# Decay rows of the state-space scan: transposed once per layer and read back from DRAM, in place of four transposes per head

## The chip, the cores and the metric

The kernel runs on one core of one Trainium2 chip. The metric is the time of one execution in microseconds, as the median of several runs. A core has TensorE (matrix multiplication, results in PSUM), VectorE, ScalarE, GpSimd and SyncE. Here SyncE issues every data transfer; 16 DMA engines carry them out. TensorE reads SBUF and writes PSUM, and GpSimd's work in this kernel is all on SBUF.

## What is computed

Two layers of a decoder trunk. Each layer projects its input once, sends parts of the projection through three branches (latent attention, a delta-rule recurrence, a state-space scan), gates and adds the branches, and ends with a feed-forward block. The change lies in the scan:

```python
a_cs = jnp.cumsum(da, axis=-1)                 # running decay sums per head
decay_in = jnp.exp(segsum(da))                 # exp(a_cs[l] - a_cs[s]) for l >= s
cb = jnp.einsum('bclgn,bcsgn->bgcls', cm, bm)
y_diag = jnp.einsum('bgcls,bgecls,bcsgep->bclgep', cb, decay_in, x)
```

There are 16 heads of 64 channels in 2 groups and 512 tokens. The kernel takes all 512 tokens as one chunk.

## The kernel before

Tokens are handled in four chunks of 128 (NC4 = 4, P = 128, S = 512). Products with weights are made from three passes each: every weight tile `wraw` of 512 KB is loaded by SyncE, rounded by ScalarE into `wH` (L231), and VectorE keeps the remainder in `wL` (L232); a projection (`proj`, L265, tile `pj`) is 24 matmuls of 512 columns. There are two raw buffers and three of each split.

In the stage of interest `mixer` interleaves three generators by a fixed pattern (`PAT`): `ssm` (the scan), `mla_attn` (attention: scores `sc`, softmax `P`, transposes `pT`, output `o`) and `gate` projections; after the attention the scan goes on beside the merging of the other branches (`rest`, `merge_two`: tiles `of`, `oH`, `oL`, `br`, `th`).

`ssm_dt` computes the step sizes and the decays on small tiles of 128 tokens x 4 chunks x 16 heads; its last product is the running sum, which L964 copies into `y` (the trace calls the tile `dy`; its negative is `de`). `ssm` then works on pairs of heads: `scores(g)` makes for each group the matrix `CB` from two convolved projections (`Bm`, `Cm`); `decays(i)` convolves a projection to `xs`, transposes it (`xT`, L1014) and scales it into `X` (L1016), and for each of the two heads builds the decay matrix `E`: running sums along the free axis, on all partitions (`ab`, L1023 to L1025), a minimum with the sum of the row's own token (L1028, VectorE), four exponentials of 128 columns (L1030) and three of 384, 256 and 128 (L1033) on ScalarE, and the product with `CB` (L1036: VectorE for the first head of a pair, GpSimd for the second). There are three buffers `E`. `out(i)` multiplies `E` with `X` on TensorE (`y`, L1049), then gates the result with another projection (`z`) and sums squares on GpSimd (L1058, L1064).

The rows `ab` come from `bcast_rows`: a column of 128 tokens, repeated along the free axis by its access pattern, goes through a TensorE transpose (L280), which leaves the column as a row on all 128 partitions in PSUM. That is four transposes for a head. The PSUM pool of the scan has three banks.

The order of the instructions on each engine is made by a planner when the program is built: it goes by the order of the program text and by its own estimates of when operands and buffers are ready, so instructions of different generators are interleaved. SyncE's transfers are in such an order too, and an instruction whose operands are not ready holds up all behind it on its engine.

Of the kernel before, what the change touches and what calls it, by code (L numbers as in the profile page):

```python
# [8 lines left out]
F32 = mybir.dt.float32  # L9
# [8 lines left out]
P = 128  # L18
S = 512
D = 1024  # L20
KD = D // P
NC4 = S // P
# [33 lines left out]
class Kern:  # L56
# [875 lines left out]
    def ssm_dt(self, T):  # L932

        nc = self.nc
        ps = self.pss.tile([P, S], F32, name="dtT", tag="r")
        for c in range(NC4):
            nc.tensor.transpose(out=ps[:, 16 * c:16 * c + 16], in_=self.krd[32:48, c * P:(c + 1) * P],
                                identity=self.ident[32:48, 32:48])
        x, e, u, y, g = (T(n, [P, NC4, 16]) for n in ("dx", "de", "du", "dy", "dg"))
        hb = lambda j: self.hrow[:, j:j + 1, :].to_broadcast([P, NC4, 16])  # L940
        nc.vector.tensor_tensor(out=x, in0=ps[:, 0:64].rearrange("p (c h) -> p c h", c=4), in1=hb(0), op=ALU.add)

        nc.vector.scalar_tensor_tensor(out=u, in0=x, scalar=-1.0, in1=x, op0=ALU.mult, op1=ALU.max)
        nc.scalar.activation(out=e, in_=u, func=AF.Exp, scale=-1.0)
        nc.vector.tensor_scalar(out=u, in0=e, scalar1=2.0, scalar2=None, op0=ALU.add)
        nc.vector.reciprocal(out=u, in_=u)
        nc.vector.tensor_tensor(out=e, in0=e, in1=u, op=ALU.mult)
        nc.vector.tensor_tensor(out=y, in0=e, in1=e, op=ALU.mult)
        nc.vector.tensor_scalar(out=g, in0=y, scalar1=1.0 / 15, scalar2=1.0 / 13, op0=ALU.mult, op1=ALU.add)
        for n in (11, 9, 7, 5, 3, 1):  # L950
            nc.vector.tensor_tensor(out=g, in0=g, in1=y, op=ALU.mult)
            nc.vector.tensor_scalar(out=g, in0=g, scalar1=1.0 / n, scalar2=None, op0=ALU.add)
        nc.vector.tensor_tensor(out=g, in0=g, in1=e, op=ALU.mult)
        nc.vector.tensor_scalar(out=x, in0=x, scalar1=0.0, scalar2=None, op0=ALU.max)
        nc.vector.scalar_tensor_tensor(out=x, in0=g, scalar=2.0, in1=x, op0=ALU.mult, op1=ALU.add)
        nc.vector.tensor_tensor(out=u, in0=x, in1=hb(1), op=ALU.mult)
        nc.vector.tensor_scalar(out=x, in0=x, scalar1=0.5, scalar2=None, op0=ALU.mult)
        ps = self.pss.tile([P, S], F32, name="acs", tag="r")
        nc.vector.memset(g[:, 0], 0.0)
        for c in range(1, NC4):  # L960
            nc.vector.tensor_tensor(out=g[:, c], in0=g[:, c - 1], in1=u[:, c - 1], op=ALU.add)
        for i, (m, t) in enumerate(((self.mle, u), (self.ones128, g))):
            nc.tensor.matmul(out=ps[:, 0:64], lhsT=m, rhs=t.rearrange("p c h -> p (c h)"), start=i == 0, stop=i == 1)
        nc.vector.tensor_copy(out=y, in_=ps[:, 0:64].rearrange("p (c h) -> p c h", c=4))  # L964
        nc.vector.tensor_scalar(out=e, in0=y, scalar1=-1.0, scalar2=None, op0=ALU.mult)
        return x, y, e

    def conv_silu(self, pg, j, out):
# [15 lines left out]
    def ssm(self, T):  # L984
        nc, l = self.nc, self.l
        PS = lambda name: self.pss.tile([P, S], F32, name=name, tag="r")
        pg = lambda name, bufs=2: T(name, [P, S], bufs)
        off = [S, S + 384, S + 640]
        dth, acs, nacs = self.ssm_dt(T)
        CB, X, xs, E, ys = {}, {}, {}, {}, {}  # L990

        def scores(g):
            Bm, Cm = pg("Bm", 1), pg("Cm", 1)
            self.conv_silu(pg, 8 + g, Bm)
            yield
            self.conv_silu(pg, 10 + g, Cm)
            cb = CB[g] = T(f"CB{g}", [P, 1280])
            for k in range(NC4):
                w = S - k * P
                ps = PS("cb")  # L1000
                nc.tensor.matmul(out=ps[:, 0:w], lhsT=Bm[:, k * P:(k + 1) * P], rhs=Cm[:, k * P:S], start=True, stop=True)
                nc.vector.scalar_tensor_tensor(out=cb[:, k * P:(k + 1) * P], in0=ps[:, 0:P], scalar=0.25, in1=self.mle,
                                               op0=ALU.mult, op1=ALU.mult)
                if k < 3:
                    nc.scalar.activation(out=cb[:, off[k]:off[k] + w - P], in_=ps[:, P:w], func=AF.Copy, scale=0.25)
            yield

        def decays(i):
            g = i // 4
            x = xs[i] = pg("xs")  # L1010
            self.conv_silu(pg, i, x)
            ps = PS("xT")
            for c in range(NC4):
                nc.tensor.transpose(out=ps[:, c * P:(c + 1) * P], in_=x[:, c * P:(c + 1) * P], identity=self.ident)  # L1014
            X[i] = T("X", [P, NC4, 2, 64], 2)
            nc.vector.tensor_tensor(  # L1016
                out=X[i].rearrange("p c h n -> p c (h n)").rearrange("p c (h n) -> p c h n", h=2),
                in0=ps.rearrange("p (c h n) -> p c h n", c=4, h=2),
                in1=dth[:, :, 2 * i:2 * i + 2].rearrange("p c (h o) -> p c h o", o=1).to_broadcast([P, NC4, 2, 64]), op=ALU.mult)
            E[i] = []  # L1020
            for hp in range(2):
                h = 2 * i + hp
                pa = PS("ab")  # L1023
                for c in range(NC4):
                    self.bcast_rows(pa[:, c * P:(c + 1) * P], acs[:, c, h:h + 1])  # L1025
                e = T("E", [P, 1280], EB)
                v4 = lambda t: t[:, 0:S].rearrange("p (c t) -> p c t", c=NC4)
                nc.vector.tensor_tensor(out=v4(e), in0=v4(pa), in1=acs[:, :, h:h + 1].to_broadcast([P, NC4, P]), op=ALU.min)  # L1028
                for k in range(NC4):
                    nc.scalar.activation(out=e[:, k * P:(k + 1) * P], in_=e[:, k * P:(k + 1) * P], func=AF.Exp,  # L1030
                                         bias=nacs[:, k, h:h + 1])
                for k in range(3):
                    nc.scalar.activation(out=e[:, off[k]:off[k] + S - (k + 1) * P], in_=pa[:, (k + 1) * P:S], func=AF.Exp,  # L1033
                                         bias=nacs[:, k, h:h + 1])
                eng = nc.gpsimd if hp else nc.vector
                eng.tensor_tensor(out=e, in0=e, in1=CB[g], op=ALU.mult)  # L1036
                E[i].append(e)
            yield
# [28 lines left out]
        def normed(g):  # L1067
# [6 lines left out]
            for j in range(4 * g, 4 * g + 4):  # L1074
                nc.vector.scalar_tensor_tensor(out=ys[j], in0=ys[j], scalar=self.dv[:, 30 + j:31 + j], in1=pb,
                                               op0=ALU.mult, op1=ALU.mult)
                nc.sync.dma_start(out=self.od["ssm"][j], in_=ys[j])

        yield from scores(0)
        yield from decays(0)  # L1080
        for i in range(8):
            if i == 3:
                yield from scores(1)
            if i < 7:
                yield from decays(i + 1)
            if i == 4:
                normed(0)
            yield from out(i)
# [281 lines left out]
```

## Time and profile before

| | |
|---|---|
| median of 3 runs | 2142.03 us (2141.42 to 2143.43) |
| the profiled execution | 2140.08 us, span of the profile 2138.1 us |
| TensorE busy | 2076.2 us, 97% |
| VectorE, ScalarE, GpSimd busy | 63%, 43%, 15% |
| mean DMA rate | 109 GB/s |

Times in the profile are counted from the start of its span. PE is TensorE's matmuls, PEld its weight loads, DVE is VectorE, ACT ScalarE, POOL GpSimd, SPq the queue of SyncE. A row of a group gives instructions of one line and form; `a<-b` names the tile written and the tiles read. The chain that ended last is followed back from the last instruction, at each step to what released it or to the instruction before it on its engine. Matmuls overlap: the time from the start of one to the start of the next is less than a matmul's own duration.

### The profile page before, as it was taken

How to read it: one execution, taken by the hardware profiler on the slowest of the kernel's cores; microseconds unless marked ns; L12 is line 12 of the kernel's file. 1: busy time of each engine (PE TensorE's matmuls, PEld its weight loads, DVE VectorE, ACT ScalarE, POOL GpSimd, SP SyncE). 2: the span in 40 equal slices, each digit the busy share in tenths (PEclk: the TensorE clock that was granted, in tenths of full speed). 3: DMA queues.
4: the chain of work that ended last, by engine and by line, in shares of the span. 5: the costliest groups of instructions: out<-in, count | busy, mean ns of one | idle time of the engine just before them, and what ended most of it. 6: DMA issues, size and time to landing. Idle time of an engine off the chain costs nothing.

```text
span 2138.1 us, 30818 instructions
## 1 busy us (share of the span) xinstructions
PE 2076.2 (97%) x12104; PEld 1650.6 (77%) x12104; DVE 1343.9 (63%) x2290; ACT 926.3 (43%) x1594; POOL 328.2 (15%) x240
## 2 busy tenths in 40 slices
PE   8999999999999999999999999999999999999999
PEld 6777777677778888888877777777677788888887
DVE  6886887877666543443557878777775654444434
ACT  5445534664433433333344454356644334333332
POOL 1001020212212111111111011002123111111120
PEclk9999999999999999999999999999999999999999
DMA  5331333124364232322332322322333632222332
GB/s 189 103 110 63 102 114 112 50 86 131 127 223 128 89 101 99 99 97 92 124 119 77 113 74 87 124 82 70 104 133 109 226 123 94 94 99 99 99 97 90
DMA packets 95616, 232.67 MB, mean 109 GB/s; under 512 B 17744, under 2 KB 27088, under 8 KB 95472
## 3 DMA queue, kind: packets, MB, share of 16 engines
q1 hardware_dynamic: 95472, 230.71, 33.1%
q8 instruction: 95, 1.56, 0.3%
q14 instruction: 49, 0.40, 0.1%
HBM read 197.64 MB, written 33.03 MB: 108 GB/s over the span
## 4 chain that ended last, share of the span: by engine, by line
PE 72%; DVE 11%; ACT 4%; issue 3%; DMA 2%; POOL 1%; SPq 0%; DVEq 0%; ACTq 0%; POOLq 0%
PE pj L265 35%; PE pf L265 16%; PE br L265 6%; PE wo L265 4%; DVE wL L232 2%; PE y L1049 2%; PE sc L898 1%; PE up L265 1%; ACT wH L231 1%; PE pT L916 1%; DMA wraw<-in_w 1%; PE YS L647 1%; DMA of<-o_ssm 1%; DVE CW L599 1%; PE o L924 1%
## 5 line engine op out<-in xcount | busy, mean ns | idle before, releaser
L265 PE MATMUL pj<-hH,wH 128*128 128x512 f32 (+1 forms) x1536 | 615.5, 401 | 7.4 <-ACT hH L234 7.4
L265 PE MATMUL pj<-hL,wH 128*128 128x512 f32 (+1 forms) x1536 | 613.0, 399 | 0.2
L265 PE MATMUL pj<-hH,wL 128*128 128x512 f32 (+1 forms) x1536 | 611.5, 398 | 0.9 <-DVE wL L232 0.9
L231 ACT CAST wH<-wraw 128x1024 fp32r<-128x1024 f32 (+1 forms) x314 | 327.4, 1043 | 655.3 <-PE pj L265 288.3
L232 DVE TENSOR_TENSOR wL<-wraw,wH 128x1024 fp32r<-128x1024 f32 (+1 forms) x314 | 415.1, 1322 | 143.2 <-ACT wH L231 142.8
L265 PEld LDWEIGHTS pj<-hH,wH 128*128 128x128 f32 (+1 forms) x1536 | 290.4, 189 | 73.9 <-ACT hH L234 7.4
L265 PEld LDWEIGHTS pj<-hL,wH 128*128 128x128 f32 (+1 forms) x1536 | 290.8, 189 | 65.0 <-issue 4.6
L265 PEld LDWEIGHTS pj<-hH,wL 128*128 128x128 f32 (+1 forms) x1536 | 290.2, 189 | 65.7 <-issue 3.3
L265 PE MATMUL pf<-uH,wH 128*128 128x512 f32 x512 | 199.2, 389 | 0.0
L265 PE MATMUL pf<-uL,wH 128*128 128x512 f32 x512 | 199.2, 389 | 0.0
L265 PE MATMUL pf<-uH,wL 128*128 128x512 f32 x512 | 199.2, 389 | 0.0
L333 POOL TENSOR_TENSOR u<-u,rsb 128x512 f32<-128x512 f32 x64 | 111.5, 1743 | 496.2 <-ACT u L332 474.5
L348 DVE TENSOR_TENSOR x<-x,pf 128x512 f32<-128x512 f32 x128 | 88.1, 688 | 139.0 <-PE pf L265 136.9
L232 DVE TENSOR_TENSOR uL<-u,uH 128x512 fp32r<-128x512 f32 x64 | 44.1, 692 | 138.1 <-ACT uH L231 138.1
L265 PEld LDWEIGHTS pf<-uH,wH 128*128 128x128 f32 x512 | 96.1, 188 | 20.0
L265 PEld LDWEIGHTS pf<-uH,wL 128*128 128x128 f32 x512 | 96.1, 188 | 20.0
L265 PEld LDWEIGHTS pf<-uL,wH 128*128 128x128 f32 x512 | 96.1, 188 | 19.9
L265 PE MATMUL br<-oH,wH 128*128 128x512 f32 x256 | 102.0, 399 | 6.4 <-ACT oH L231 6.4
L265 PE MATMUL br<-oL,wH 128*128 128x512 f32 x256 | 101.9, 398 | 4.3 <-DVE oL L232 4.3
L1036 POOL TENSOR_TENSOR E<-E,CB 128x1280 f32<-128x1280 f32 x16 | 48.7, 3045 | 353.5 <-ACT E L1033 310.7
L265 PE MATMUL br<-oH,wL 128*128 128x512 f32 x256 | 101.1, 395 | 0.0
L335 ACT ACTIVATE u<-u 128x512 f32<-128x512 f32 x64 | 40.5, 633 | 119.1 <-POOL u L333 119.1
(364 smaller groups left out, 2820.9 us busy)
## 6 DMA issues: line engine op xcount, KB each, us to landing
wraw<-in_w SPq DMA_DIRECT2D x302, 512.0 KB, 3.4
gd<-gt SPq DMA_DIRECT2D x48, 256.0 KB, 2.1
th<-gd SPq DMA_DIRECT2D x16, 512.0 KB, 3.9
xd<-x SPq DMA_DIRECT2D x8, 512.0 KB, 5.8
o_ssm<-ys SPq DMA_DIRECT2D x16, 256.0 KB, 2.1
x<-xd SPq DMA_DIRECT2D x8, 512.0 KB, 5.8
of<-o_ssm SPq DMA_DIRECT2D x16, 256.0 KB, 4.3
t<-gd SPq DMA_DIRECT2D x16, 256.0 KB, 2.7
```

Source lines behind the costliest of these rows:

```text
L231: nc.scalar.copy(out=H, in_=src)
L232: nc.vector.tensor_tensor(out=Lo, in0=src, in1=H.bitcast(F32), op=ALU.subtract)
L265: nc.tensor.matmul(out=ps, lhsT=ww if w_is_lhs else aa, rhs=aa if w_is_lhs else ww, start=first and k == 0 and q == 0, stop=last and k == ...
L333: nc.gpsimd.tensor_tensor(out=u, in0=u, in1=self.rsb, op=ALU.mult)
L335: nc.scalar.activation(out=u2, in_=u, func=AF.Square)
L348: nc.vector.tensor_tensor(out=xk, in0=xk, in1=ps, op=ALU.add)
L599: nc.vector.tensor_tensor(out=CW[o, hp], in0=pv[o], in1=mk, op=ALU.mult)
L647: nc.tensor.matmul(out=pS[m, 256 * hp + i * 64:256 * hp + i * 64 + 64], lhsT=LT[h, hp, i, m], rhs=Z[h, hp, i], start=True, stop=True)
L898: nc.tensor.matmul(out=ps[:, 0:w], lhsT=fT[0][:, j * P:w], rhs=fT[1][:, 0:w], start=True, stop=True)
L916: nc.tensor.transpose(out=ps[:, (j - k) * P:(j - k + 1) * P], in_=Pj[hp][j][:, k * P:(k + 1) * P], identity=self.ident)
L1036: eng.tensor_tensor(out=e, in0=e, in1=CB[g], op=ALU.mult)
L1049: nc.tensor.matmul(out=py[64 * hp:64 * hp + 64, t0:t1], lhsT=X[i][:, k, hp, :], rhs=m, start=k == 0, stop=(d == 0), skip_group_check=True)
```

## The change

`ssm_dt` also transposes the running sums, `y`, once per layer: four transposes of 128 tokens x 16 heads give a tile of 16 x 512 in PSUM; ScalarE copies it to SBUF, into one of the two buffers of the convolution's tile `cy`, and SyncE stores it to DRAM as `acd`. `decays(i)` begins with two loads that each read one row of `acd` and repeat it on all 128 partitions (256 KB written per load), into one of three buffers `ar`; the four transposes for each head are gone, and the minimum and the exponentials of L1033 read `ar` in SBUF instead of PSUM. The two tiles `CB0` and `CB1` become one tile `CB` with one buffer, which both groups use in turn.

```diff
@@ ssm_dt
         nc.vector.tensor_scalar(out=e, in0=y, scalar1=-1.0, scalar2=None, op0=ALU.mult)
+
+        ps = self.pss.tile([P, S], F32, name="aT", tag="r")
+        for c in range(NC4):
+            nc.tensor.transpose(out=ps[0:16, c * P:(c + 1) * P], in_=y[:, c, :], identity=self.ident)
+        at = T("cy", [P, S], 2)[0:16]
+        nc.scalar.copy(out=at, in_=ps[0:16])
+        self.acd = self.dram.tile([16, S], F32, name=f"acd{self.l}")
+        nc.sync.dma_start(out=self.acd, in_=at)
         return x, y, e
@@ scores
-            cb = CB[g] = T(f"CB{g}", [P, 1280])
+            cb = CB[g] = T("CB", [P, 1280])
@@ decays
             x = xs[i] = pg("xs")
+            rows = [T("ar", [P, S], 3) for _ in range(2)]
+            for hp in range(2):
+                h = 2 * i + hp
+                nc.sync.dma_start(out=rows[hp], in_=self.acd[h:h + 1].to_broadcast([P, S]))
             self.conv_silu(pg, i, x)
@@ decays, for each head
-                pa = PS("ab")
-                for c in range(NC4):
-                    self.bcast_rows(pa[:, c * P:(c + 1) * P], acs[:, c, h:h + 1])
+                pa = rows[hp]
                 e = T("E", [P, 1280], EB)
```

## Rows read from the trace of the kernel before

**Rows 1.** The page: busy us by engine (share, instructions); the chain by engine.
```profile
PE 2076.2 (97%) x12104; PEld 1650.6 (77%) x12104; DVE 1343.9 (63%) x2290; ACT 926.3 (43%) x1594; POOL 328.2 (15%) x240
...
PE 72%; DVE 11%; ACT 4%; issue 3%; DMA 2%; POOL 1%; SPq 0%; DVEq 0%; ACTq 0%; POOLq 0%
```

**Rows 2.** Windows, the scan's two stretches: busy us (instructions), clock, DMA share, GB/s.
```profile
340.00:600.00 260.00, 252.94 (x1359) 191.00 (x1358) 196.88 (x358) 143.19 (x317) 52.82 (x27) 1.00 0.30 97
1420.00:1660.00 240.00, 233.42 (x1268) 175.33 (x1267) 179.67 (x341) 135.93 (x308) 52.68 (x26) 1.00 0.29 95
```

**Rows 3.** Tile ab: count, min/median/max ns, first and last start, forms.
```profile
L280 PE MATMUL ab<-ident,dy x128: 272/273/273, 367.5 to 1629.3; 128*128 128x128 f32 x128
L1033 ACT ACTIVATE E<-ab,de x96: 350/458/572, 370.2 to 1635.8; 128x384 f32<-128x384 f32 x32, 128x256 f32<-128x256 f32 x32, 128x128 f32<-128x128 f32 x32
```

**Rows 4.** Timeline of TensorE around one group: start us, us, instruction.
```profile
405.32 1.04 PE L280 MATMUL ab<-ident,dy 128*128 128x128 f32 x8
406.20 1.02 PE L898 MATMUL sc<-kh,qh 96*128 96x512 f32 x2
```

**Rows 5.** Chain that ended last, first and last group of transposes: start us, us.
```profile
405.49 0.87 PE ab L280 x8
...
1628.66 0.87 PE ab L280 x8
```

**Rows 6.** Chain at layer 0's first pair.
```profile
368.40 0.61 DVE E L1028
...
374.56 2.41 DVE P L905
```

**Rows 7.** Tile E: the exponentials from SBUF, whole span.
```profile
L1030 ACT ACTIVATE E<-E,de x128: 384/388/407, 369.0 to 1634.6; 128x128 f32<-128x128 f32 x128
```

**Rows 8.** Chain at layer 0's sixth pair.
```profile
511.11 0.69 DVE E L1028
...
515.71 2.58 DVE E L1036
```

**Rows 9.** Timeline of VectorE: sums written and first minima, layer 0, then layer 1.
```profile
357.57 0.21 DVE L964 COPY dy<-acs 128x64 f32<-128x64 f32 x1
...
368.32 1.28 DVE L1028 TENSOR_TENSOR E<-ab,dy 128x512 f32<-128x512 f32 x2
...
1432.80 0.22 DVE L964 COPY dy<-acs 128x64 f32<-128x64 f32 x1
...
1435.24 1.28 DVE L1028 TENSOR_TENSOR E<-ab,dy 128x512 f32<-128x512 f32 x2
```

**Rows 10.** Layer 1's first pair: timeline of GpSimd, then the chain on TensorE.
```profile
1440.65 2.88 POOL L1036 TENSOR_TENSOR E<-E,CB 128x1280 f32<-128x1280 f32 x1 [72.23 <-ACT E L1033]
...
1446.17 1.01 PE y L1049 x6
```

**Rows 11.** A ScalarE copy (timeline); DMA issues: count, KB each, median us to landing.
```profile
361.27 0.58 ACT L891 COPY qh<-qh 96x512 f32<-96x512 f32 x1
...
gd<-gt SPq DMA_DIRECT2D x48, 256.0 KB, 2.1
of<-o_ssm SPq DMA_DIRECT2D x16, 256.0 KB, 4.3
o_rwkv<-o SPq DMA_DIRECT2D x16, 128.0 KB, 2.2
```

**Rows 12.** Waits of SyncE's queue, 1420 to 1660 us: total us, times, longest.
```profile
SPq L241 <- DVE wL L232: 128.2, 19, 31.5
```

**Rows 13.** Chain of layer 1 where it passes a weight load.
```profile
1596.70 4.97 DMA wraw<-in_w
```

**Rows 14.** VectorE alone and beside GpSimd products (timelines; GpSimd's second from the chain).
```profile
365.69 0.69 DVE L982 SCALAR_TENSOR_TENSOR xs<-th,cy 128x512 f32<-128x512 f32 x1
1441.47 2.61 DVE L982 SCALAR_TENSOR_TENSOR xs<-th,cy 128x512 f32<-128x512 f32 x1
...
1590.53 3.45 POOL E L1036
1591.08 0.67 DVE L1127 SCALAR_TENSOR_TENSOR th<-th,br 128x512 f32<-128x512 f32 x1
```

## Prediction

> **What bounds the kernel now.** I read the busy table of the page first. TensorE is busy for 97% of the span, and 72% of the chain that ended last lies on it; ScalarE has 4% of the chain against 43% busy [rows 1]. Then the two stretches that hold the scan, one in each layer: TensorE is busy 252.9 of 260 us and 233.4 of 240 us, VectorE about three quarters, the DMA engines 30% [rows 2]. So work taken from TensorE should shorten the stage, unless its work there is partly waiting for another engine. The other three views are the row of the removed instructions, the chain step by step, and the order of the SyncE queue.
>
> **The transposes that go.** There are 128 of them, 8 for each of the 8 head pairs in each of 2 layers, 273 ns each [rows 3]; 128 x 0.273 = 34.9 us looks like the prize and is not, because matmuls overlap. The timeline shows what a group of 8 occupies: it starts at 405.32 and TensorE starts the next work at 406.20, 0.88 us later [rows 4]. So 16 groups hold TensorE for about 16 x 0.88 = 14.1 us at most. On the chain that ended last the program's own pieces are 0.87 us a group, and only 11 of the 16 groups are on it, the first at 405.49 and the last at 1628.66 [rows 5]: 11 x 0.87 = **-9.6 us**. The other five lie beside a chain on other engines: at layer 0's first pair it runs through VectorE's minimum at 368.40 and on to a VectorE scaling that ends at 376.97 [rows 6]. For those five I take nothing; if they counted too the removal would be worth 14.1.
>
> **What is added on TensorE.** Four transposes of the 16 columns of a chunk, once per layer. Half of a group of 8 is 0.44 us, twice is 0.9: **+0.9 us**. Nothing hides it, TensorE being the bound; zero if it falls into one of the stage's gaps.
>
> **The operand that moves.** The minimum (L1028) and the exponentials at L1033 now read SBUF instead of PSUM. For the exponentials the trace has both: a 128x128 one from SBUF takes 384 ns at least (L1030) and from PSUM 350 (L1033) [rows 3, 7], so 96 of them cost 96 x 0.034 = 3.3 us of ScalarE, between 0 and 3.3 on the end. I take ScalarE's share of the chain over its busy share, 4/43 of it [rows 1]: **+0.3 us**. For the minimum the duration itself should stay at 0.68 us, a guess that the rival on the port below tests.
>
> **The wait that goes.** The minimum no longer waits for TensorE. In one place this lies on the chain: minimum at 511.11, then the exponentials, then the product that starts at 515.71 [rows 8]. If all of that can be done before the projection arrives, up to 4.6 us go; zero if VectorE and ScalarE merely do it at another time. They are busy there with other work that is needed just as much, so I take **-1.0 us**.
>
> **The first pair of each layer** gets a longer path. Before, the sums were in SBUF and then 8 transposes. Now come four transposes (0.44), a copy by ScalarE (0.58 for 96x512), a store, and a load of 256 KB that waits for the store to land; stores and loads of 128 to 256 KB land 2.1 to 4.3 us after issue [rows 11]. So 0.44 + 0.58 + 2.1 + 2.1 = 5.2 us at least and 0.44 + 0.58 + 4.3 + 4.3 = 9.6 at most. In layer 0 the sums are written at 357.57 + 0.21 and the minimum starts at 368.32, 10.5 us later [rows 9]: hidden. In layer 1 they are written at 1432.80 + 0.22 and the minimum starts at 1435.24, 2.2 us later [rows 9], so it comes 3.0 to 7.4 us late. The last product of that pair ends at 1440.65 + 2.88 = 1443.5 on GpSimd and TensorE takes it up at 1446.17 [rows 10], a slack of 2.6. The delay is then 0.4 to 4.8 us, if TensorE finds nothing else; it has a projection and attention to go on with. Behind the late minimum VectorE holds the attention's scaling and the next convolution, which the planner can put ahead of it: in the best case the 4.6 us of exponentials leave the front of ScalarE's queue and something is gained, -1. I take **+1.0 us**, near the lower end, because of that other work. The copy borrows one of the two convolution buffers `cy`, which at worst holds back the second of the two convolutions of the scores by the time of the store; that lies inside the same bound.
>
> **The SyncE queue.** Per layer one store and 16 loads of 256 KB each, 4 MB in 250 us, so 17 GB/s beside the 97 that move there [rows 2]. All of SyncE's transfers pass through one queue in order, weight loads too, and it stands still up to 31.5 us on a weight load that waits for VectorE [rows 12]. A row load waits for one of three buffers `ar`, and everything behind it waits with it: weight loads, gate stores, the loads of the branch outputs. By the code the first row of a pair finds a buffer that was last read a pair and a half earlier; the second needs the exponentials of the pair just before, which end some 5 us after its minimum (1435.24 to 1440.65 for a first pair [rows 9, 10]), while eight pairs share a stretch of 240 us or more. Cost taken: 0, hidden under the head start of the weight loads; the price without it is a rival. One buffer `CB` for both groups makes the second scores wait for the products of the fourth pair; two projections lie in between, nothing.
>
> **The sum** is -9.6 + 0.9 + 0.3 - 1.0 + 1.0 = -8.4 us. Against the profiled execution's 2140.1 us (span 2138.1) that gives 2131.7; the median of the three runs is 2142.0, 1.9 above that execution, so **2133.6 us**, -0.39%. What this kernel's measurement can tell from no change is about 0.2%, 4.3 us: faster is below 2137.7, slower above 2146.3.
>
> **Rivals.**
> *TensorE is the only bound.* All 16 groups count, since TensorE is 97% busy in both stretches [rows 2]: -14.1 + 0.9 = -13.2, so 2128.8. Against it: the chain leaves TensorE at five of the groups.
> *Other links take over.* TensorE gets to its projections earlier, but their weights are split by VectorE and ScalarE in the same order as before, and those two are the chain around the first pair [rows 6]. If 8 of the 11 groups only lengthen a wait, 7.0 of the 9.6 go back: -1.4, so 2140.6, no change that can be measured.
> *The row loads hold back the weights* (slower). Place: SyncE, at each of the 14 pairs that need a buffer back. In layer 1 the chain runs through a weight load at 1596.70, 4.97 us long [rows 13], so a late weight load there costs one for one. If each of the 14 puts d us on the end, it decides from 8.4/14 = 0.6 us on; at 1.0 us the total is +14 - 8.4 = +5.6, 2147.6. Against it: the buffers come free early, as said above, and only one such load is on the chain.
> *The shared port.* A VectorE instruction with both operands in SBUF stretches while GpSimd computes: the last step of a convolution takes 0.69 us, and 2.61 beside a GpSimd product that had begun at 1440.65 [rows 10, 14]; one that reads PSUM took its 0.67 us beside another product [rows 14]. The minimum changes from the second kind to the first. In before none of the 32 minima runs beside a GpSimd instruction, because the product comes after the pair's exponentials. If the new order puts a third of them there, 10 x 1.9 us are 19 us of VectorE, of which half may reach the end: +9.5 - 8.4 = +1.1, 2143.1, no change. The Trainium skill, "SBUF — State Buffer", section "Who interferes with whom", states this as a rule against the change: a VectorE instruction with two SBUF inputs is blocked by a GpSimd one that reads SBUF, one with a single SBUF input is not. The trace agrees with both halves, by the durations just given.
>
> **How the numbers follow.** Chances: the forecast (2130 to 2137.7) 0.40, TensorE alone 0.22, other links 0.19, weights held back 0.13, the port 0.06. Faster: 0.40 + 0.22 = 0.62; within 0.2%: 0.19 + 0.06 = 0.25; slower: 0.13. The range goes from 2126, where TensorE alone and some of the 4.6 us of the freed wait meet, to 2146, past the port and at the edge of the held-back weights.
>
> **What will show it.** In the changed kernel the row of the 128 transposes is gone, and 8 in all of the new kind stand in their place; TensorE's busy time falls by about 13 us, and the span by about 8. Minima beside GpSimd products show the port; waits of projections on weights, or of weight splits on loads, show the third rival; the first minimum of layer 1 some 3 to 7 us after where it stood shows the new path. The prediction is wrong if the stretches don't shorten, or if the order of the attention against the projections changes so much that the chain passes other places.

## The result, and the profile after

The changed kernel takes 2161.4 us, the median of four runs (2159.6 to 2165.5), against 2142.7 for the kernel before on the same chip (four runs): a ratio of 1.0085, 95% interval 1.007 to 1.010. It is slower by about 19 us, where the forecast was 8.4 us faster and the range ended at 2146. The profiled execution took 2162.1 us, its span is 2160.4.

The page of the changed kernel, busy time by engine and then the chain by engine (before: [rows 1]):

```profile
PE 2083.1 (96%) x11984; PEld 1647.5 (76%) x11984; DVE 1351.1 (63%) x2290; ACT 930.9 (43%) x1596; POOL 326.9 (15%) x240
...
PE 71%; DVE 12%; ACT 3%; issue 3%; DMA 3%; POOL 1%; SPq 0%; DVEq 0%; ACTq 0%; POOLq 0%
```

The transposes are gone: 120 fewer matmuls, as 128 went and 8 came. Yet TensorE is busy for 2083.1 us, where some 13 us less than 2076.2 were forecast. So I cut both traces at the same work: from the start of the 889th projection matmul to the 1489th, which holds layer 0's scan, and from the 3265th to the 3793rd, which holds layer 1's. The windows of before, between these marks (length, then busy us of PE, PEld, DVE, ACT, POOL, then granted clock, DMA share, GB/s); they add to 500.1, with TensorE busy for 486.5:

```profile
341.00:599.70 258.70, 251.64 (x1354) 189.92 (x1352) 196.60 (x356) 142.91 (x317) 52.75 (x26) 1.00 0.30 97
1420.70:1662.10 241.40, 234.82 (x1276) 176.49 (x1273) 179.55 (x340) 136.06 (x309) 52.68 (x26) 1.00 0.29 95
```

And of the changed kernel, between the same marks, with their sum:

```profile
338.60:609.80 271.20, 256.12 (x1293) 189.71 (x1292) 193.77 (x356) 144.90 (x318) 52.96 (x26) 0.97 0.35 108
1433.90:1684.70 250.80, 237.01 (x1215) 173.81 (x1213) 190.20 (x335) 139.90 (x312) 51.43 (x26) 0.98 0.34 109
sum 522.00, PE 493.13 PEld 363.52 DVE 383.97 ACT 284.80 POOL 104.39; mean PE 246.56 PEld 181.76 DVE 191.99 ACT 142.40 POOL 52.19
```

The two stretches are 21.9 us longer, nearly all of the 22.3 between the two spans. Three entries make most of it. The removal counts -13.2 (16 x 0.88 less, 0.9 more for the new transposes). TensorE stands idle for 522.0 - 493.1 = 28.9 us in place of 13.6: +15.3. And the granted clock, 1.00 in both stretches of before, falls in seven windows of 10 us of the changed kernel, of which these are three; the four that are left out, at 430, 550, 1480 and 1620, have 0.83 each:

```profile
390.00:400.00 10.00, 6.53 (x32) 4.54 (x29) 4.38 (x8) 5.15 (x12) 2.80 (x2) 0.82 0.34 102
400.00:410.00 10.00, 10.00 (x40) 7.30 (x40) 7.62 (x21) 4.99 (x11) 0.00 (x0) 0.84 0.32 105
...
1460.00:1470.00 10.00, 6.25 (x27) 3.21 (x28) 8.88 (x22) 4.08 (x10) 0.00 (x0) 0.83 0.10 23
```

The missing parts add to 7 - 5.81 = 1.19 windows: 11.9 us of TensorE's time at 2.4 GHz, lost to moments at 1.2. That is a bound for what they cost, since TensorE was idle in some of these windows. The three give -13.2 + 15.3 + 11.9 = 14.0 of the 21.9; the other 8, or more if the clock's part is smaller, lie in time in which TensorE counts as busy. The matmuls of y alone are busy 11.6 us longer, part of it at the lower clock, as the rows under the hold below show.

Why TensorE waits is seen in the chain of the changed kernel at layer 0's second pair (start us, us, what):

```profile
387.22 4.34 POOL E L1046
391.56 1.25 POOL ys L1068
...
392.83 0.04 ACT yac L1072
...
393.37 0.97 ACT E L1040 x3
394.34 1.20 ACT E L1043 x3
395.53 0.47 ACT qh L891
396.00 0.59 ACT kh L893
...
396.64 2.93 PE sc L898 x6
```

Read it from the end. The scores of an attention head wait for the copy of `kh`, which stands on ScalarE behind the last six exponentials of pair 2's first head (its minimum is at 386.98). These stand behind the square of pair 0's gated output, and the square waits for GpSimd's gate product, which stands behind GpSimd's product of pair 1. Neither is needed yet: pair 1's y begins at 412.35, pair 2's at 442.65. In before GpSimd had these two the other way round (timeline of GpSimd):

```profile
388.29 1.41 POOL L1058 TENSOR_TENSOR ys<-ys,th 128x512 f32<-128x512 f32 x1 [11.61 <-DVE ys L1052]
390.34 3.56 POOL L1036 TENSOR_TENSOR E<-E,CB 128x1280 f32<-128x1280 f32 x1 [0.64 <-ACT E L1033]
```

The largest wait of TensorE in the changed kernel, 335 to 620 us (us in total, times, longest), is this link; in before it has 0.2 us there:

```profile
PE sc L898 <- ACT kh L893: 8.5, 3, 3.5
```

In layer 1 the same link holds TensorE for 0.8 us only. The longest wait there, 3.75 us up to 1464.20, ends with an exponential of the attention's softmax, so one link does not explain both layers.

Pair 1 could come so early because its rows were there. Layer 0's minima of pairs 1 to 4 began, by the starts of the score matmuls, after 15, 30, 46 and 64 of the layer's 64 in before, and after 0, 16, 32 and 48 now. So the planner puts decays about one attention step ahead, and they then wait for an `E` buffer: the engines that read the tile `ar` in the changed kernel sat idle 36.4 us, 23 times, until y had given one back. In before it was 11.1 us, 6 times, on the tile `ab`. The rows of the changed kernel, then that one of before:

```profile
L1043 ACT ACTIVATE E<-ar,de x96: 384/495/618, 357.9 to 1656.6; 128x384 f32<-128x384 f32 x32, 128x256 f32<-128x256 f32 x32, 128x128 f32<-128x128 f32 x32
L1038 DVE TENSOR_TENSOR E<-ar,dy x32: 679/692/1789, 358.5 to 1654.5; 128x512 f32<-128x512 f32 x32
  PE y L1059: 36.4, 23
DMA to landing us min/median/max: 3.1/3.3/4.7
```

```profile
  PE y L1049: 11.1, 6
```

### The profile page after: what moved, and what is told of

It reads as the page before. It is cut to its first block, busy times and chain, and to the rows that moved or that the text cites. A ratio compares the mean times of both kernels' runs of the same rounds, so it can differ in the third digit from the quotient of the medians.

```text
span 2160.4 us, 30678 instructions
## 1 busy us (share of the span) xinstructions
PE 2083.1 (96%) x11984; PEld 1647.5 (76%) x11984; DVE 1351.1 (63%) x2290; ACT 930.9 (43%) x1596; POOL 326.9 (15%) x240
## 4 chain that ended last, share of the span: by engine, by line
PE 71%; DVE 12%; ACT 3%; issue 3%; DMA 3%; POOL 1%; SPq 0%; DVEq 0%; ACTq 0%; POOLq 0%
PE pj L265 34%; PE pf L265 16%; PE br L265 6%; PE wo L265 4%; PE y L1059 2%; DVE wL L232 2%; PE sc L898 2%; PE up L265 1%; DMA of<-o_ssm 1%; PE pT L916 1%; DMA wraw<-in_w 1%; DVE cy L987 1%; PE YS L647 1%; DVE Xt L687 1%; ACT wH L231 1%
## 5 line engine op out<-in xcount | busy, mean ns | idle before, releaser
L232 DVE TENSOR_TENSOR uL<-u,uH 128x512 fp32r<-128x512 f32 x64 | 44.1, 692 | 138.1 <-ACT uH L231 138.1
```

The source lines that it names most:

```text
L232: nc.vector.tensor_tensor(out=Lo, in0=src, in1=H.bitcast(F32), op=ALU.subtract)
```

## The experiments

Theory Q: the loss is the planner's new order; early rows let it put decays ahead, in queues that run in order, of work for which TensorE waits sooner. Rival L: the row loads hold back the weights. All ratios are to the kernel before on the same chip (its medians were 2139.9 to 2142.5). The changed kernel itself was timed on one chip only, and the groups of runs on others, so differences between groups, and to its 2161.4, are safer by the ratios than by the medians. The runs without loads and e4_one_transpose use a constant row: they price time and compute other decays.

| run | edit | median us | ratio, 95% interval |
|---|---|---|---|
| e1_hold | changed, decays held | 2139.4 | 0.998 (0.9963 to 0.9997) |
| e2_no_loads | changed, no loads | 2156.6 | 1.008 (1.0054 to 1.0106) |
| e2h_no_loads_hold | both | 2135.2 | 0.9968 (0.9953 to 0.9983) |
| e3_loads_too | before, with loads | 2148.8 | 1.0039 (1.0024 to 1.0053) |
| e4_one_transpose | before, 32 of 128 transposes | 2129.2 | 0.9943 (0.9924 to 0.9962) |
| e5_hold_act | changed, ScalarE held | 2150.4 | 1.0046 (1.0031 to 1.006) |
| e6_hold_pool | changed, GpSimd held | 2155.0 | 1.0065 (1.0039 to 1.0091) |
| e7_hold_y | held, y kept together | 2140.7 | 0.9992 (0.9973 to 1.0011) |
| e8_rows_by_matmul | rows by a matmul | 2145.5 | 1.0024 (1.0009 to 1.0039) |
| e9_three | no loads, 3 buffers E | 2155.6 | 1.0067 (1.0043 to 1.0091) |
| e9_four_buffers | no loads, 4 buffers E | 2162.7 | 1.0105 (1.0076 to 1.0134) |
| e10_later | changed, decays written later | 2141.9 | 1.0003 (0.9987 to 1.0019) |
| e11_later_still | later still | 2140.1 | 1.0006 (0.9991 to 1.0021) |
| e12_first_pair | e10, first pair by transposes | 2164.1 | 1.0109 (1.0088 to 1.0131) |
| e13_later_no_loads | e10, no loads | 2145.0 | 1.002 (1.0005 to 1.0035) |
| e14_hold_first | held, first pair by transposes | 2143.4 | 1.0016 (0.9997 to 1.0035) |
| e15_hold_pool_too | held, GpSimd held too | 2136.5 | 0.9984 (0.9963 to 1.0004) |

### Order or loads: a square of four

The hold is two ordering edges, with no wait and no other data (`tanh` is the convolution's, `xm` the X multiply; the other exponentials stand in the same block):

```
-            self.conv_silu(pg, i, x)
+            tanh = self.conv_silu(pg, i, x)
...
-            nc.vector.tensor_tensor(
+            xm = nc.vector.tensor_tensor(
...
+                with self.tc.issue_after(xm.ins):
+                    nc.vector.tensor_tensor(out=v4(e), in0=v4(pa), in1=acs[:, :, h:h + 1].to_broadcast([P, NC4, P]), op=ALU.min)
+                with self.tc.issue_after(tanh):
+                    for k in range(NC4):
+                        nc.scalar.activation(out=e[:, k * P:(k + 1) * P], in_=e[:, k * P:(k + 1) * P], func=AF.Exp,
...
```

> Edit: the changed kernel, in which each pair's minimum is queued behind that pair's X multiply on VectorE and its exponentials behind that pair's convolution tanh on ScalarE, places like those they had while the transposes tied them to TensorE; loads, data and waits are the same. Theory Q (the rows' early arrival lets the planner place the next pair's decays ahead of the previous pair's gate, and the queues of ScalarE and GpSimd then stand still until the product y frees an E buffer): the loss goes, 2130 to 2140 us, and TensorE's scores no longer wait for the kh copy. Rival L (the row loads, their traffic or their place in SyncE's queue hold back the weights): nothing of this changes, 2155 us or more.

Without the loads:

```
-            rows = [T("ar", [P, S], 3) for _ in range(2)]
-            for hp in range(2):
-                h = 2 * i + hp
-                nc.sync.dma_start(out=rows[hp], in_=self.acd[h:h + 1].to_broadcast([P, S]))
+            rows = [fix, fix]
...
+        fix = T("fix", [P, S])
+        nc.vector.memset(fix, -1.0e4)
```

> Edit: the changed kernel without the row loads: the minimum and the exponentials read one SBUF tile set once per layer to a constant, so the decays are not the reference's; the four transposes of the sums, the copy and the store stay. The decays now depend on nothing but buffers. Theory Q: still slow, 2150 to 2165 us, since the early decays still take the queues. Rival L: the loss goes with the loads, 2130 to 2140.

> Edit: both of the two edits before this: no row loads (constant rows, so the decays are not the reference's) and the minimum and exponentials queued behind the pair's X multiply and tanh. Its difference to the kernel with the hold alone is what the 32 loads cost at this order. Theory Q: 0 to 3 us below that kernel, so 2128 to 2140. Rival L: 15 us or more below it, about 2130.

With the changed kernel's 2161.4 the four make a square. The hold is worth 22.0 us with the loads and 2156.6 - 2135.2 = 21.4 without (22 and 24 by the ratios). Taking the loads away is worth 4.8 and 4.3 by the medians, 1.1 and 2.6 by the ratios, and the intervals overlap. So the first half of Q is shown: the loss comes with the planner's order, since two edges that change nothing else take it away. L falls for the bulk of it: the kernel without a single row load is as slow, within 5 us. The single `CB`, the store of the sums and the operand in SBUF are in the held kernel too, so they do not make the loss either. What in the order costs the time is a second question. The sum over the same two stretches of the held kernel:

```profile
sum 499.20, PE 483.51 PEld 356.12 DVE 377.22 ACT 283.58 POOL 100.44; mean PE 241.75 PEld 178.06 DVE 188.61 ACT 141.79 POOL 50.22
```

Its timeline of ScalarE where the changed kernel had six exponentials between the square and the copies:

```profile
394.59 0.63 ACT L1075 ACTIVATE yac<-ys 128x512 f32<-128x512 f32 x1 [3.84 <-POOL ys L1071]
395.12 0.56 ACT L891 COPY qh<-qh 96x512 f32<-96x512 f32 x1
395.59 0.68 ACT L893 ACTIVATE kh<-kh,dv 96x512 f32<-96x512 f32 x1
```

GpSimd's product still stands ahead of the gate at this pair (389.72 and 393.27), but no exponentials stand behind the square. The scores' wait for the copy of `kh` in layer 0 falls from 8.5 us to 3.0; it was expected to go. Yet e2_no_loads, which is slow, has 3.2 us of it. So this link shows how the changed kernel loses time at one place, and it is not what the slow orders have in common. The held kernel, then e2_no_loads, 335 to 620 us:

```profile
PE sc L898 <- ACT kh L893: 3.0, 3, 1.4
```

```profile
PE sc L898 <- ACT kh L893: 3.2, 3, 2.3
```

TensorE's idle time in the held kernel is 499.2 - 483.5 = 15.7 us, near before's 13.6, and the clock's loss is 1.7 us, in two windows. But the hold only brings the stretches to 499.2, 0.9 under before, where -13.2 + 2.1 + 1.7 = -9.4 were due. The other 8.5 us are again busy time of TensorE, and up to 6.7 of them belong to y. The sums of the same stretches for the tile `y` alone, before, then held, then changed:

```profile
sum 500.10, PE 40.79 PEld 27.46 DVE 11.77; mean PE 20.39 PEld 13.73 DVE 5.89
```

```profile
sum 499.20, PE 47.45 PEld 28.25 DVE 11.82; mean PE 23.73 PEld 14.13 DVE 5.91
```

```profile
sum 522.00, PE 52.37 PEld 30.93 DVE 11.80; mean PE 26.19 PEld 15.47 DVE 5.90
```

In before a pair's matmuls of y run nearly as one block, which the changed kernel mixes with the attention's transposes (timelines of TensorE; pair 2 in before, then pair 1 in the changed kernel):

```profile
437.29 2.38 PE L1049 MATMUL y<-E,X 128*64 128x128 f32 x26
439.60 0.44 PE L916 MATMUL pT<-ident,P 128*128 128x128 f32 x2
439.97 0.43 PE L1049 MATMUL y<-E,X 128*64 128x128 f32 x2
```

```profile
412.35 0.43 PE L1059 MATMUL y<-E,X 128*64 128x128 f32 x2
412.71 0.66 PE L916 MATMUL pT<-ident,P 128*128 128x128 f32 x4
413.30 0.87 PE L1059 MATMUL y<-E,X 128*64 128x128 f32 x4
414.10 0.88 PE L916 MATMUL pT<-ident,P 128*128 128x128 f32 x6
414.90 1.08 PE L1059 MATMUL y<-E,X 128*64 128x384 f32 x8
415.91 0.44 PE L916 MATMUL pT<-ident,P 128*128 128x128 f32 x2
416.28 0.87 PE L1059 MATMUL y<-E,X 128*64 128x256 f32 x8
417.07 0.44 PE L916 MATMUL pT<-ident,P 128*128 128x128 f32 x2
417.44 0.65 PE L1059 MATMUL y<-E,X 128*64 128x128 f32 x6
```

28 matmuls of y are busy 2.81 us in the first and 3.90 in the second. A part of that is counted twice: a group's last matmul still runs when the next group starts (412.35 + 0.43 lies past 412.71). I asked whether that mixing is a cause or only a place where a wait shows, by starting y with the head that comes last:

```
-                    for hp in range(2):
+                    for hp in (1, 0):
...
+                        if first is None:
+                            first = mm()
+                        else:
+                            with self.tc.issue_after(first):
+                                mm()
```

> Edit: the held kernel (minimum and exponentials queued behind the pair's X multiply and tanh) in which each pair's matmuls of y start with the second head, whose product is GpSimd's and last, and all others are queued behind that first one. In the held kernel 7 of 32 half groups have other work between the two heads' matmuls, which otherwise start 0.01 us apart. If that broken pairing is where the saved transposes went: 3 to 8 us below the held kernel, 2131 to 2136. If it is only another place of the same waits: within 2 us of it, 2137 to 2141.

y's share fell from 47.5 to 44.1 us and the two stretches did not get shorter (500.4). So the mixing is not shown to be a cause: the second expectation, another place of the same waits, fits better, though the intervals of the two runs overlap. What takes its turn is not settled.

### The loads alone, and the transposes alone

To the kernel before I added the transposes of the sums, their copy and store and the single `CB`, as the change has them, and the loads:

```
+            rows = [T("ar", [P, S], 3) for _ in range(2)]
+            for hp in range(2):
+                h = 2 * i + hp
+                nc.sync.dma_start(out=rows[hp], in_=self.acd[h:h + 1].to_broadcast([P, S]))
```

> Edit: the kernel before with all its transposes, to which the store, the 32 row loads into three buffers (read by nothing but the next load's buffer rule) and the single CB buffer are added. The load's buffer comes free as soon as the load before it landed, so this prices the traffic, the store's wait and the issues on SyncE, not a wait for a reader. Theory Q: 2140 to 2147, as before. Rival L by traffic: 2152 us or more; if the price is the wait for a reader, this run doesn't show it.

6.4 us by the medians (8.4 by the ratio), between the two theories. Its own added transposes and copy are in it, and the planner's order changed too, so it only says that the loads and what belongs to them are worth a few us.

And from the kernel before I took three of four transposes:

```
-                for c in range(NC4):
-                    self.bcast_rows(pa[:, c * P:(c + 1) * P], acs[:, c, h:h + 1])
+                self.bcast_rows(pa[:, 0:P], low)
...
-                nc.vector.tensor_tensor(out=v4(e), in0=v4(pa),
+                nc.vector.tensor_tensor(out=v4(e), in0=pa[:, 0:P].rearrange("p (o t) -> p o t", o=1).to_broadcast([P, NC4, P]),
```

> Edit: the kernel before with one transpose per head in place of four, its 128 columns read four times by the minimum and by the other exponentials; the column is a constant, so the decays are not the reference's. 96 of 128 transposes go, 16 x 0.66 = 10.6 us of TensorE; the decays still wait for TensorE, and no row is loaded. The step of the sum that counts 11 of 16 groups: -7.3 us against before, about 2135. TensorE as the only bound: -10.6, about 2132. Theory O (the stage's other engines are as late as TensorE, so the time saved becomes waits): 0 to -4, 2138 to 2143.

-12.2 us by the ratio's 0.9943 (interval -16.3 to -8.1). This is what the rival "TensorE is the only bound" says, 10.6 for all 16 groups; the 7.3 of 11 groups lies outside the interval. But the planner had a free hand here too, so a part of it may be a luckier order, and one kernel does not tell the two apart. The sum over its stretches: TensorE's idle time even falls, to 488.2 - 477.4 = 10.8 us.

```profile
sum 488.20, PE 477.38 PEld 356.99 DVE 377.48 ACT 279.17 POOL 101.91; mean PE 238.69 PEld 178.50 DVE 188.74 ACT 139.59 POOL 50.95
```

So TensorE's time was to be had while the decays still waited for TensorE; with early rows it was lost, and more.

### Which part of the order

ScalarE alone keeps one of the hold's two edges:

```
+                with self.tc.issue_after(tanh):
+                    for k in range(NC4):
...
```

> Edit: the changed kernel in which only the exponentials are held, behind the pair's convolution tanh on ScalarE; the minimum on VectorE and the product on GpSimd are free. If ScalarE's queue is where the early decays do their harm: as with both held, 2135 to 2143. If VectorE's minimum ahead of other work carries part of it: 2145 to 2158.

GpSimd alone has its product moved into the step of its pair's y:

```
+            if i:
+                with self.tc.issue_after(gate[i - 1]):
+                    nc.gpsimd.tensor_tensor(out=E[i][1], in0=E[i][1], in1=CB[g], op=ALU.mult)
             py = PS("y")
```

> Edit: the changed kernel in which only GpSimd's order is set: the product for the second head of a pair is queued behind the gate product of the pair before; the minima and exponentials stay as early as the planner puts them. If the harm is that the gate, and with it ScalarE's square and all that is queued behind it, stands behind a product which waits for a late E: most of it goes, 2138 to 2148. If the harm is that minima and exponentials waiting for an E buffer block VectorE and ScalarE themselves: 2152 to 2162.

Holding ScalarE alone gives back 11 of the 22 us (8 by the ratios), setting GpSimd's order alone 6 (4 by the ratios, and its interval overlaps that of the changed kernel). So the gate's delay is not the main thing, and neither queue is shown to be the place alone. The rest of the hold is the minimum's place on VectorE; its share is argued and not shown, since the planner orders everything else anew in each run. The narrow form of Q says that decays harm because they wait for y in the queues; a fourth buffer tests it:

```
-WB, WR, EB = 3, 2, 3
+WB, WR, EB = 3, 2, 4
...
+        fix = T("fix", [P, P])
```

> Edit: as the kernel without loads, but the constant rows are one 128x128 tile read several times (the decays are not the reference's); three buffers for E, as in the changed kernel. It is the control for the next one. Expected like the kernel without loads: 2150 to 2160 us.

> Edit: as the control (no loads, constant rows, so the decays are not the reference's), with four buffers for E in place of three, so that a pair's two decays can be built while the two of the pair before are still read. Theory Q in its narrow form (the decays, placed early, stand in the queues until y frees the third buffer): the waits of ScalarE and VectorE for y go, and the time falls to 2128 to 2140. If early decays harm only because they are put ahead of the attention's copies and scalings, whatever they wait for: 2148 to 2160, as with three.

The narrow form fell: 2162.7, above the three buffers' 2155.6, with intervals that overlap. VectorE's minima still waited 8.1 us for y in layer 0, in 4 places where three buffers had 7, and the decays came earlier still. Room for more early work does not help, so the wait for the buffer is a companion and not the cause.

Next I moved the decays in the program, without any edge:

```
         def out(i):
+            if i < 7:
+                exps(i + 1)
             py = PS("y")
```

`exps` is the loop with minimum, exponentials and products, which stood in `decays`; in the second run it stands behind the gate and the square of `out`.

> Edit: the changed kernel, in which minimum, exponentials and products of pair i+1 are written down one step later in the program, at the start of the step that holds pair i's y, not behind pair i+1's convolution; the planner is free, nothing else is changed. In before the minimum of a pair starts with 15, 30, 46 and 64 of the 64 score matmuls of the layer begun (pairs 1 to 4), in the changed kernel with 0, 16, 32 and 48. Theory S (a step too early is the whole harm): the counts come back to about before's, and the time is that of the held kernel or better, 2130 to 2141. If the early rows let the planner put them early anyhow: 2150 or more.

> Edit: as the one before, but minimum, exponentials and products of pair i+1 stand behind pair i's gate and square in the program, half a step later. Theory S: 2130 to 2143 too, better if the gate had to come first (GpSimd's order), worse if pair i+1's y now waits for its decays, 2143 to 2150.

Both are at before's time: 20 us came back from the place in the program alone. But the reason I gave is wrong: layer 0's first minima of pairs 1 to 4 still begin after 0, 16, 32 and 48 scores, as in the changed kernel, and the readers of `ar` still wait 23.3 and 28.9 us for y. So neither early minima nor their wait is by itself the loss. On top of the first of these, two more, the first of them with this edit, the second with the constant rows of e2_no_loads:

```
-                pa = rows[i][hp]
+                pa = rows[i][hp] if i else PS("ab")
+                if not i:
+                    for c in range(NC4):
+                        self.bcast_rows(pa[:, c * P:(c + 1) * P], acs[:, c, h:h + 1])
...
-            for hp in range(2):
+            for hp in range(2 if i else 0):
```

> Edit: as the first of these (decays one step later in the program), and the first pair of each layer takes its rows by eight transposes as in before, so it waits for no store and no load. If the first pair's longer path costs what the prediction put at 1.0 (0.4 to 4.8) us: 1 to 5 us below the first of these, less 1.8 for its 16 transposes. If it is covered: 0 to 2 us above it.

> Edit: as the first of these (decays one step later in the program), without row loads: constant rows, so the decays are not the reference's; the transposes, copy and store of the sums stay. The loads cost 4.8 us at the early order and 4.3 at the held one; if that is their price at any order, 3 to 6 us below the first of these, so 2126 to 2136. If it was the order that each build happened to get: between 2 above and 2 below.

The first pair's rows by transposes, a change of one pair in eight, lost 22 us again, which neither expectation had. Its sums beside those of the kernel it was made from (e10_later first) have the marks of the changed kernel, 27.4 us of idle TensorE against 21.6. The profiled execution of e10_later is its fastest, 2134.7, and its stretches are still 6.4 us longer than before's, so in it not all of the 20 us came back in these stretches:

```profile
sum 506.50, PE 484.86 PEld 358.63 DVE 377.46 ACT 285.04 POOL 105.90; mean PE 242.43 PEld 179.31 DVE 188.73 ACT 142.52 POOL 52.95
```

```profile
sum 522.20, PE 494.77 PEld 366.10 DVE 388.75 ACT 283.69 POOL 98.93; mean PE 247.39 PEld 183.05 DVE 194.38 ACT 141.84 POOL 49.46
```

And without the loads this order is 3.1 us slower, with overlapping intervals, where 3 to 6 us less or no change were expected. So with early rows the planner's result jumps by some 20 us on small edits, and a price of a few us, such as that of the loads, can't be read from a single pair of such kernels. Whether the hold guards against the jump was the last question, asked with the same edit of the first pair in the held kernel, and with GpSimd's edit of e6_hold_pool beside the hold:

> Edit: the held kernel (minimum and exponentials queued behind the pair's X multiply and tanh), in which the first pair of each layer takes its rows by eight transposes as in before, waiting for no store and no load. If the hold keeps the planner from the slow order: the price of the first pair's longer path, 0.4 to 4.8 us by the prediction, less 1.8 for 16 transposes, so 2136 to 2141. If a small edit still tips the planner, hold or not: 2150 or more, as it did without the hold.

> Edit: the held kernel, in which GpSimd's product for the second head of a pair is also queued behind the gate product of the pair before. In the held kernel that product stands ahead of the gate at some pairs, and the gate waits some 4 us for it. If the gate's delay (and the square and copies behind it on ScalarE) still costs: 2 to 6 us below the held kernel, 2133 to 2138. If the hold had already taken it away: 2138 to 2142; if y now waits for the product that was put back: 2142 to 2150.

It does, as far as these go: five kernels with the hold lie between 2135 and 2144, among them the one with the edit that tipped e10_later. That one, 2143.4, is between its two expectations; it gained nothing against 2139.4 by giving the first pair its transposes back. GpSimd's edit is 2.9 us under the held kernel by the medians and not by the ratios, so nothing is shown for it. e15_hold_pool_too, 2136.5, and e1_hold are the fastest versions that compute the reference's decays: 0.2% under before, the first with an interval that reaches 1.0004, the second with one that ends at 0.9997. Both beat the changed kernel by 22 us or more and before by hardly what can be told.

### Rows by one matmul

```
-                nc.sync.dma_start(out=rows[hp], in_=self.acd[h:h + 1].to_broadcast([P, S]))
+                nc.tensor.matmul(out=pa, lhsT=sel[:, h:h + 1].to_broadcast([48, P]), rhs=at, start=True, stop=True)
```

> Edit: the sums are transposed once per layer as in the changed kernel, but not stored: they stay in SBUF as a rounded part and its rest, on 48 partitions, and one matmul of 128x512 per head against a column of ones and zeros writes the row onto all partitions in PSUM, where four transposes stood. No row is loaded, and the decays wait for TensorE as before. A pair's two matmuls take about 2 x 0.23 us (the spacing of the 128x512 matmuls of the projections) where eight transposes took 0.88: 16 x 0.42 = 6.7 us less, 0.9 more for the transposes of the sums. Theory Q (the loss is in the order, which this leaves alone): -3 to -8 us against before, so 2133 to 2138, and below the held kernel. If any change of TensorE's load in this stage lets the planner put the decays early again: 2145 or more.

A miss, 2145.5, though no row comes early. The first term was sized wrong: two such matmuls start at 409.87 and the next work at 410.52, 0.65 us a pair and not 0.46, so eight transposes for two matmuls save 0.23 a pair, 3.7 in all less 0.9. The rest is not explained. In the profiled execution, which at 2152.1 is slower than the median, layer 0's stretch is 1.6 us shorter than in before, layer 1's 4.8 longer, and 9 us more lie outside both.

## Why the prediction was wrong, step by step

**The wait that goes** is the step that failed. It booked -1.0 us for a minimum that no longer waits for TensorE, on the ground that at worst VectorE and ScalarE would do the same work at another time, with zero as the worst end. What another time can cost had no term. The wait had also fixed an order; without it the planner made one in which TensorE stands idle for 28.9 us in place of 13.6 and loses up to 11.9 to the clock. Tying minimum and exponentials back takes off 22 us, with the loads and without, so the square of four puts the loss on this step, which the prediction had bounded from one side only. How the order costs is shown at one place, where decays stand ahead of a copy that TensorE waits for; two kernels with minima as early are at before's time. Its own last sentence named the case, "if the order of the attention against the projections changes so much that the chain passes other places", but gave it no price and no chance. The Trainium skill, "PSUM — Partial Sum Buffer", section "Engine vs sequencer instructions", calls the queues of ScalarE, VectorE and GpSimd strict FIFO; the chain above agrees, a copy of 0.47 us at 395.53 that stands behind 2.2 us of exponentials.

**The transposes that go** were perhaps undersized: 11 of 16 groups by the chain, where the run with one transpose per head gained as much as all of them would, in an order of its own. A chain that leaves TensorE at five groups need not mean that TensorE's time is free there.

**The operand that moves**: the exponentials at L1043 take 384 to 618 ns where [rows 3] has 350 to 572 from PSUM, 34 to 46 more each, close to the 34 that were taken.

**The first pair.** From the sums to the first minimum, timelines of VectorE and SyncE in the changed kernel:

```profile
349.53 0.22 DVE L964 COPY dy<-acs 128x64 f32<-128x64 f32 x1 [0.78 <-PE acs L963]
353.71 1.43 SPq L1022 DMA_DIRECT2D ar<-acd  x3
358.54 0.68 DVE L1038 TENSOR_TENSOR E<-ar,dy 128x512 f32<-128x512 f32 x1
1438.86 0.23 DVE L964 COPY dy<-acs 128x64 f32<-128x64 f32 x1
1450.62 0.69 DVE L1038 TENSOR_TENSOR E<-ar,dy 128x512 f32<-128x512 f32 x1
```

8.8 us in layer 0, inside the 5.2 to 9.6 of the working, and 11.5 in layer 1, above it ([rows 9] has 10.5 and 2.2): the minimum comes 9.3 us late there, where 3.0 to 7.4 were forecast. The run that gave the first pair its transposes back under the hold gained nothing, so no cost of the longer path is seen there.

**The SyncE queue** was costed at 0. The queue's waits in the changed kernel, 338 to 610 us, then in before, 340 to 600:

```profile
SPq L241 <- DVE wL L232: 97.5, 20, 14.0
SPq L1022 <- DVE E L1038: 27.5, 8, 12.4
SPq L1022 <- ACT E L1043: 26.9, 8, 6.7
```

```profile
SPq L241 <- DVE wL L232: 132.8, 20, 28.2
```

Row loads do stand there for 54 us in this layer, while the weight loads' wait falls from 132.8 us to 97.5. What the loads cost is 4.8 and 4.3 us by the medians at two orders and -3.1 at a third, none of them clear of the intervals; beside before's transposes, with the rest of the change, 6.4. The 14 us of the slower rival are not seen.

**The port**: in the changed kernel 5 of the 32 minima are stretched, to between 1.39 and 1.79 us, each begun while a GpSimd instruction ran. That is 4.3 us of VectorE in all, where that rival had 19.

What stays open: which part of the order decides. More buffers, GpSimd's order alone and ScalarE's alone do not bring the time back, and minima as early as in the slow kernel go with before's time. And in the held kernel 8.5 us of TensorE's freed time do not come back.

## What to carry to other kernels

A wait that is taken away also takes away an order. Before booking it at zero or as a gain, ask which instructions may now start earlier, what stands behind them on each in-order engine, and who waits for that; under a planner that orders by readiness, bound it on the losing side too. Where an early operand is wanted for its own sake, keep the consumers where they were by an ordering edge, and then measure. Their place in the program did it here too, but a change of one pair tipped it back.

## What was not expected of the hardware

A row of 2 KB in DRAM, read onto all 128 partitions as 256 KB, landed 3.1 to 4.7 us after issue, median 3.3, between the store and the load of that size in [rows 11]. And a wait of TensorE cost more than its length. Each of the six falls of the clock inside the two stretches of the changed kernel comes at the end of a time without work of 2.3 to 3.8 us, or just behind it. After the 3.47 us that end at 396.64 the granted clock is 0.82 and 0.84 in the windows on both sides, and six score matmuls are busy 2.93 us; in before, where both windows have 1.00, the same six take 1.57:

```profile
396.44 1.57 PE L898 MATMUL sc<-kh,qh 96*128 96x128 f32 x6
```
